# A hybrid attention and RWKV-7 layer on one core: the recurrence's chunk products on four quadrants of the array, and another road from the out projection into the FFN

## The chip, the cores and the metric

The kernel runs on one core of a Trainium2 chip. The metric is the device time of one execution in microseconds (us), lower is better; the time of a kernel is the median over its runs. Five engines work side by side and wait for one another through semaphores: TensorE (PE, with its weight loads listed apart as PEld), VectorE (DVE), ScalarE (ACT), GpSimd (POOL) and SyncE (SP), which issues most of the DMAs. Each engine goes through its own list of instructions in order, so an instruction that waits holds up everything behind it on that engine.

## The reference

One decoder layer over 1024 tokens of width 1024, all in float32. Half of the mixer's channels go through dilated attention (8 heads of 64), half through an RWKV-7 recurrence (8 heads of 64); both halves are joined, multiplied by an output matrix, normed and added to x; then comes an FFN from 1024 to 4096 and back.

```python
def step(state, inp):                       # RWKV-7, per head; state is 64 x 64
    r_t, w_t, k_t, v_t, kk_t, b_t = inp
    sa = einsum('bhij,bhj->bhi', state, kk_t)
    state = state * w_t[:, :, None, :] - sa[..., None] * b_t[:, :, None, :] + v_t[..., None] * k_t[:, :, None, :]
    return state, einsum('bhij,bhj->bhi', state, r_t)
...
mixed = concatenate([attn, rw], axis=-1) @ w_out
x = x + rms_norm(mixed, norm_mix_post)
h = rms_norm(x, norm_ffn_pre)
f = square(relu(h @ w_ffn_up)) @ w_ffn_down
x = x + rms_norm(f, norm_ffn_post)
```

where `rms_norm(x, g) = x / sqrt(mean(x*x) + 1e-6) * g`.

## The kernel before, in words

**Products.** A product of the projections is three matmuls (`mm3`: high times high, low times high, high times low), whose operands are split into a high and a low part; ACT writes the high part and DVE subtracts for the low one. `mm` records every matmul, so most matmuls of the program stand under one line (L47; L49 in the changed kernel). The small products of the recurrence are plain float32 matmuls, which the array runs as more than one instruction each.

**Projections and recurrence, 80 to 444 us of the span.** The sequence is cut into 16 chunks of 64 tokens, and the 8 RWKV heads are taken as 4 pairs; a pair's two heads lie in the two halves of the 128 partitions (`own[0]`, `own[1]`). Each pair goes through four jobs: `norms` (key norms, into the bank `pst`), `pre_pair` (decays, the chunk matrices N from the product `pN`, L436, and the spill of N), `subst` (solves small triangular blocks on DVE and writes them to `z_d`) and `merge` (L496): it loads Z from `z_d` (L502), transposes it to X (L503), multiplies N by X (`qu1`, L511) and the result W by Z (`qu2`, L519), merges again in 32x32 blocks (`qu3`, `qu4`), and stores to `zp_d` (L538), which `unit_e` needs later. `pN`, `qu1` and `qu2` are 32 products of 64x64 by 64x64 for each pair. In each, one head's operands and result lie in the upper half of the partitions, the other's in the lower: of the four 64x64 quadrants of the array the two on the diagonal take turns. After the pairs come eight units of 128 tokens: `unit_ab` and `unit_e` prepare the matrices, and `unit_c` (L624 on) walks the chunks one after the other, `O` from HV, then VU on ACT (L635), `O` from VU, then HV for the next chunk on DVE (L641, L642). That walk is serial.

**What sets the order there.** The six big projections (`z_k`, `z_r`, `z_v` for the recurrence, `z_aq`, `z_ak`, `z_av` for attention) are cut into 24 slabs of 48 matmuls. They are independent of the recurrence and are laid between its steps as filler. A planner, `drive` (L754), writes the order of PE and SP: it keeps a clock `now`, adds a cost for each step of a job (the first number of each `yield`) or 0.7 for three filler matmuls, and lets a job's next step in when its due time is past; due times come from the table `WAIT` or the default behind the `yield`. The last slabs (`aq3`, `ak3`, `av3`) may only start after the last chunk. DVE, ACT and POOL are ordered by the scheduler of the tile framework, by priority.

**Out projection and FFN, 618 us on.** The out projection goes by 8 token blocks of 128 (`half_mm`, 24 matmuls each half, into `pm`). `mix_x1` takes a block's norm, adds x, takes the next norm and scales (`yg`); `mix_h2` transposes yg on PE into `h2t` and writes high and low parts to `HB` and the sums `T1` to `T4`, four operands of a Strassen-like FFN: products of weight blocks with HB go to banks X and Y, later ones with T2, T1, T3 and T4 to X, Y and Z. Each weight block (`up_raw`, tile `wr`, 3 buffers) is loaded by SP and split by `split_w`; `up_rest` makes weight sums s21 and s34 on DVE. The last block of tokens (`pm7`, `y7`, `yg7`, `h2t7`) ends the out projection, and the third FFN product `X2` needs it. `rstd1` is the norm: a square root on ACT, then a reciprocal and one Newton step on DVE.

Of the kernel before, what the change touches and what calls it, by code (L numbers as in the profile page):

```python
# [1 line left out]

# [38 lines left out]
def hybrid_kernel(tc, x, par, cst, strip, win, wup_lora, gup, gnwb, grow, wout, wup, wdown, out, dbg=None):  # L41
# [22 lines left out]
    with (  # L64
# [29 lines left out]
        eps1 = cp.tile([P, 1], F32, name="eps1")  # L94
        A.activation(eps1, eps, AF.Sqrt)

        def rstd1(y, ssum, nm, more=eps, more_v=-0.5 * NORM_EPS):
# [6 lines left out]
            V.tensor_tensor(m, y, y, OP.mult)
            V.tensor_tensor(m, m, v_, OP.mult)
# [390 lines left out]
        def merge(p):  # L496
# [4 lines left out]
            for h in range(2):  # L501
                nc.sync.dma_start(Z[own[h]], d_full(zd, h))  # L502
# [1027 lines left out]
```

## Time and profile before

| | us |
|---|---|
| median of 3 runs (lowest, highest) | 1339.01 (1337.86, 1342.17) |
| the profiled execution's own time | 1342.16 |
| its span | 1338.3 |
| PE busy, share of the span | 1283.8 (96%) |
| DVE busy | 902.5 (67%) |
| ACT busy | 627.8 (47%) |
| POOL busy | 40.9 (3%) |
| granted TensorE clock, mean | 0.989 |

The span runs from the first to the last recorded event; the execution's time is 3.9 us longer. Stages in the span: x and first norm to about 47 us, small projections, then the pairs with projections as filler from 80 to 305 us, the units to 444, the last slabs to 473, attention to 618, out projection to about 710, FFN up to 1045, FFN down and the final norm to the end. PE is busy nearly all the time, so what it is given to do is read as closely as where it waits.

### The profile page before, as it was taken

How to read it: one execution, taken by the hardware profiler on the slowest of the kernel's cores; microseconds unless marked ns; L12 is line 12 of the kernel's file. 1: busy time of each engine (PE TensorE's matmuls, PEld its weight loads, DVE VectorE, ACT ScalarE, POOL GpSimd, SP SyncE). 2: the span in 40 equal slices, each digit the busy share in tenths (PEclk: the TensorE clock that was granted, in tenths of full speed). 3: DMA queues.
4: the chain of work that ended last, by engine and by line, in shares of the span. 5: the costliest groups of instructions: out<-in, count | busy, mean ns of one | idle time of the engine just before them, and what ended most of it. 6: DMA issues, size and time to landing. Idle time of an engine off the chain costs nothing.

```text
span 1338.3 us, 23569 instructions
## 1 busy us (share of the span) xinstructions
PE 1283.8 (96%) x9360; PEld 1060.0 (79%) x9360; DVE 902.5 (67%) x1648; ACT 627.8 (47%) x1029; POOL 40.9 (3%) x59
## 2 busy tenths in 40 slices
PE   6899999999989989999998999999999999999997
PEld 5677888878777878787886888888888888888876
DVE  7867657632677657655879977667766776445586
ACT  7653324233455267765656443434344344443443
POOL 0000000000000000000000000000000002000211
PEclk9999989999989989999999999999999999999999
DMA  7346746877585586502433544454457984346554
GB/s 259 116 173 171 193 119 186 245 209 228 177 250 168 188 270 183 149 25 96 152 106 136 177 164 147 140 168 151 148 189 238 348 326 161 104 133 200 189 197 180
DMA packets 163757, 239.48 MB, mean 179 GB/s; under 512 B 52192, under 2 KB 89312, under 8 KB 163648
## 3 DMA queue, kind: packets, MB, share of 16 engines
q1 hardware_dynamic: 154304, 212.81, 49.8%
q10 hardware_dynamic: 8064, 20.98, 4.7%
q0 software_dynamic: 1280, 4.20, 0.8%
q8 instruction: 73, 1.20, 0.4%
q14 instruction: 36, 0.29, 0.1%
HBM read 160.85 MB, written 77.09 MB: 178 GB/s over the span
## 4 chain that ended last, share of the span: by engine, by line
PE 74%; DVE 10%; DMA 9%; ACT 5%; issue 2%; SPq 1%; DVEq 0%; ACTq 0%
PE X L47 12%; PE dX L47 8%; PE Z L47 6%; PE pm L47 6%; PE dZ L47 5%; PE dY L47 3%; PE z_aq L47 3%; PE z_r L47 3%; PE Y L47 3%; PE z_v L47 3%; PE z_ak L47 2%; PE pT L909 2%; PE po L47 2%; PE pS L47 2%; PE z_av L47 2%
## 5 line engine op out<-in xcount | busy, mean ns | idle before, releaser
L47 PE MATMUL dX<-wow,wou 128*128 128x512 f32 x768 | 176.3, 390 | 2.4 <-DVE wow L1181 2.1
L47 PEld LDWEIGHTS dX<-wow,wou 128*128 128x128 f32 x768 | 143.8, 188 | 34.3 <-DVE wow L1181 3.8
L47 PE MATMUL dZ<-wow,wou 128*128 128x512 f32 x384 | 87.4, 389 | 0.0
L1180 ACT ACTIVATE wow<-wd 128x1024 fp32r<-128x1024 f32 x40 | 42.3, 1060 | 88.7 <-PE dZ L47 29.7
L47 PEld LDWEIGHTS dZ<-wow,wou 128*128 128x128 f32 x384 | 72.1, 188 | 15.0
L1181 DVE TENSOR_TENSOR wou<-ur,wou 128x1024 fp32r<-128x1024 f32 x56 | 71.8, 1283 | 7.2 <-ACT wou L1180 7.0
L1181 DVE TENSOR_TENSOR wow<-wd,wow 128x1024 fp32r<-128x1024 f32 x40 | 49.2, 1232 | 33.8 <-ACT wow L1180 33.4
L1180 ACT ACTIVATE wou<-ur 128x1024 fp32r<-128x1024 f32 x56 | 58.6, 1049 | 21.4 <-DMA ur<-u_d 14.1
L897 DVE CUSTOM_DVE_ANT_0 S<-pS,stripT 128x512 f32<-128x512 f32 (+3 forms) x64 | 37.7, 588 | 34.7 <-PE pS L47 33.1
L899 ACT ACTIVATE S<-S,mn 128x128 f32<-128x128 f32 (+7 forms) x64 | 49.4, 772 | 15.8 <-DVE mn L897 15.3
L1268 ACT ACTIVATE r<-u 128x512 f32<-128x512 f32 x48 | 30.1, 626 | 52.4 <-DVE u L1266 52.3
L909 PE MATMUL pT<-cst,S 128*128 128x128 f32 x288 | 44.8, 284 | 7.1 <-ACT PT L911 6.0
L47 PE MATMUL pm<-WO,mxr 128*128 128x512 f32 x192 | 49.2, 400 | 0.8 <-DVE mxr L977 0.8
L1181 DVE TENSOR_TENSOR wow<-TK,wow 128x1024 fp32r<-128x1024 f32 x16 | 20.8, 1301 | 38.9 <-ACT wow L1180 38.9
L47 PE MATMUL Z<-HB,wo 128*128 128x512 f32 x192 | 46.1, 389 | 0.0
L1452 POOL TENSOR_TENSOR E<-E,gpF 128x512 f32<-128x512 f32 x12 | 21.1, 1771 | 806.5 <-DMA xf<-x_d 639.7
L47 PE MATMUL pm<-WO,mxa 128*128 128x512 f32 x192 | 45.8, 394 | 0.0
L47 PE MATMUL z_aq<-hT,wh_aq 128*128 128x512 f32 x128 | 45.5, 407 | 0.0
L47 PE MATMUL X<-HB,wo 128*128 128x512 f32 x180 | 43.6, 390 | 1.6 <-ACT HB L1039 1.6
L47 PE MATMUL z_av<-hT,wh_av 128*128 128x512 f32 x128 | 45.1, 409 | 0.0
L909 PEld LDWEIGHTS pT<-cst,S 128*128 128x128 f32 x288 | 33.6, 144 | 14.5 <-ACT PT L911 10.5
L47 PE MATMUL z_r<-hT,wh_r 128*128 128x512 f32 x128 | 44.8, 408 | 0.0
(393 smaller groups left out, 3093.4 us busy)
## 6 DMA issues: line engine op xcount, KB each, us to landing
ur<-u_d SPq DMA_DIRECT2D x56, 512.0 KB, 4.3
wd<-in_wdown_dram SPq DMA_DIRECT2D x40, 512.0 KB, 4.3
u_d<-S SPq DMA_DIRECT2D x64, 256.0 KB, 2.1
u_d<-u SPq DMA_DIRECT2D x48, 256.0 KB, 2.2
wr_upa<-in_wup_dram SPq DMA_DIRECT2D x16, 512.0 KB, 3.6
wr_upb<-in_wup_dram SPq DMA_DIRECT2D x16, 512.0 KB, 4.0
TK<-in_wdown_dram SPq DMA_DIRECT2D x16, 512.0 KB, 7.6
x<-in_x_dram SPq DMA_DIRECT2D x8, 512.0 KB, 6.9
```

The costliest lines, as they stand in the source:

```text
L47: return PE.matmul(o, lhsT, rhs, start=start, stop=stop, skip_group_check=True)
L897: V.tensor_tensor_reduce(Sx[:, lo:hi], pS[:, :hi - lo], stripT[:, so:so + hi - lo], 1.0, 3e38 if k == 0 else mn[:, 0:1], OP.add, OP.min, a ...
L899: A.activation(Sx[:, :w], Sx[:, :w], AF.Exp, scale=-1.0, bias=mn[:, nbk - 1:nbk], accum_out=at[p, "den"][:, i, h:h + 1])
L909: PE.transpose(pt[:, j], Sx[:, (4 * k + j) * P:(4 * k + j + 1) * P], ident)
L1180: A.activation(w[:, 0, 0:n], raw, AF.Copy)
L1181: E.tensor_tensor(w[:, 1, 0:n], raw, w[:, 0, 0:n].bitcast(F32), OP.subtract)
L1268: A.activation(r, src, AF.Relu)
L1452: G.tensor_tensor(e, e, gn[n], OP.mult)
```

## The change

It has two halves. In the **recurrence**:

- A new helper `turned` issues the products of `pN`, `qu1` and `qu2` two chunks at a time. An even chunk's two heads use the diagonal quadrants as before; for an odd chunk, one of the operands or the result lies in the other half of the partitions, so the other two quadrants are used. The results go to two banks, one for even and one for odd chunks.
- So odd chunks of N and X lie in the other half. N is spilled by four DMAs of half the size instead of two (`d_half`). Z is loaded by four, and two more load a copy `Zo` of the odd chunks in their own half; the copy has the buffer tag `HX` that `subst` uses for its scratch tile. The mask of N is four DVE operations of half the size, and W is evacuated by ACT (even) and DVE (odd) instead of ACT alone.
- The sums for the key norms and the bonus (`pst`, `pb`) are issued through `mm_h`, which splits each product by output columns into two halves of 64.
- The planner has other costs for these steps and another `WAIT` table.

From the **out projection to the FFN**:

- `rstd1` needs three DVE operations instead of four.
- `mix_x1` multiplies by the gain ahead of the norm, works in halves of 512, and scales `yg` half on ACT, half on DVE. `mix_h2` saves copies (T3, T4) with two ACT instructions in its first half and needs fewer DVE operations in its second.
- The transposes of block ORD[6] are laid inside the last block's out projection, after 18 of its 24 matmuls.
- Several weight splits and sums are held by `issue_after` until named instructions of block 7's or block 6's norm have been issued: W1[1], W1[2], `up_rest(0)`, and the early parts of T.
- For the first FFN block the sums s34, the low parts w3 and w4, and the low part of T4 go to GpSimd.

```diff
-WAIT = {'mrg1.0': 26.0, ... 'ab1.0': 4}
+WAIT = {'mrg1.0': 26.0, ... 'H3': 1.0}
...
-    def rstd1(y, ssum, nm, more=eps, more_v=-0.5 * NORM_EPS):
+    V.tensor_scalar(eps4, eps, 0.25, None, op0=OP.mult)
+    def rstd1(y, ssum, nm, more=eps4, more_v=0.25 * NORM_EPS):
         n = ssum.shape[1]
         sq_, v_, m = (sm.tile([P, 2], F32, name=f"r1{c_}_{nm}", tag="r1" + c_, bufs=4)[:, :n] for c_ in "svm")
-        A.activation(sq_, ssum, AF.Sqrt, scale=1.0 / D, bias=more)
-        V.tensor_scalar(v_, ssum, -0.5 / D, more_v, op0=OP.mult, op1=OP.add)
-        V.reciprocal(y, sq_)
-        V.tensor_tensor(m, y, y, OP.mult)
-        V.tensor_tensor(m, m, v_, OP.mult)
-        V.scalar_tensor_tensor(y, m, 1.5, y, OP.add, OP.mult)
+        A.activation(sq_, ssum, AF.Sqrt, scale=0.25 / D, bias=more)
+        V.tensor_scalar(v_, ssum, 0.25 / D, more_v, op0=OP.mult, op1=OP.add)
+        V.reciprocal(m, sq_)
+        if n == 1:
+            V.scalar_tensor_tensor(m, m, v_, sq_, OP.mult, OP.add)
+        else:
+            V.tensor_tensor(m, m, v_, OP.mult)
+            V.tensor_tensor(m, m, sq_, OP.add)
+        V.reciprocal(y, m)
...
-                mm(pst[:, 8 * f + 2 * t:8 * f + 2 * t + 2], sq[:, t * P:(t + 1) * P], bone)
+                mm_h(pst[:, 8 * f + 2 * t:8 * f + 2 * t + 2], sq[:, t * P:(t + 1) * P], bone)
...
+    def turned(pq, f, lhsT, rhs, rows):
+        for cc in range(0, 8, 2):
+            for r in range(2):
+                for h in range(2):
+                    i = own[h ^ (r & rows)]
+                    mm(pq[r][own[h ^ (r & (1 - rows))], 4 * f + cc // 2], lhsT(cc, r)[i], rhs(cc, r)[i])
...
-            pN = bank(f"pN{p}_{f}", "w", bufs=2)
-            for cc in range(8):
-                for h in range(2):
-                    mm(pN[own[h], cc], bk[own[h], cc, 0, :], ar[own[h], cc, 0, :])
-            V.tensor_tensor(N[:, 8 * f:8 * f + 8], pN, maskn.unsqueeze(1).to_broadcast([P, 8, 64]), OP.mult)
-            yield 1.0, (3.0, 2.5)[f]
+            pN = [bank(f"pN{p}_{f}_{r}", "w", (P, 4, 64), 2) for r in range(2)]
+            turned(pN, 0, lambda cc, r: bk[:, cc + r, 0], lambda cc, r: ar[:, cc + r, 0], 0)
+            for r in range(2):
+                V.tensor_tensor(N[:, 8 * f + r:8 * f + 8:2], pN[r], maskn.unsqueeze(1).to_broadcast([P, 4, 64]), OP.mult)
+            yield 0.7, (3.2, 2.7)[f]
         for h in range(2):
-            nc.sync.dma_start(d_full(n_d[p % 2], h), N[own[h]])
+            for r in range(2):
+                nc.sync.dma_start(d_half(n_d[p % 2], h, r), N[own[h ^ r], r::2])
...
+        Zo = c8(t5(f"Zo{p}", "HX"))
         for h in range(2):
-            nc.sync.dma_start(Z[own[h]], d_full(zd, h))
+            for r in range(2):
+                nc.sync.dma_start(Z[own[h ^ r], r::2], d_half(zd, h, r))
+            nc.sync.dma_start(Zo[own[h]], d_half(zd, h, 1))
         V.transpose(fl(X), fl(Z))
         yield 0.0, 4.0
+        pq = [bank(f"qu1_{p}_{r}", "bc"[r]) for r in range(2)]
         for f in range(2):
-            fs = slice(8 * f, 8 * f + 8)
-            pu = bank(f"qu1_{p}_{f}", "bc"[f])
-            for cc in range(8):
-                for h in (0, 64):
-                    mm(pu[h:h + 64, cc], N[h:h + 64, 8 * f + cc], X[h:h + 64, 8 * f + cc])
-            A.activation(W[:, fs], pu, AF.Copy)
-        yield 2.4, 1.5
+            turned(pq, f, lambda cc, r: N[:, 8 * f + cc + r], lambda cc, r: X[:, 8 * f + cc + r], 1)
+        A.activation(W[:, 0::2], pq[0], AF.Copy)
+        V.tensor_copy(W[:, 1::2], pq[1])
+        yield 1.3, 1.9
+        pq = [bank(f"qu2_{p}_{r}", "bc"[r]) for r in range(2)]
         for f in range(2):
-            fs = slice(8 * f, 8 * f + 8)
-            pu = bank(f"qu2_{p}_{f}", "bc"[f])
-            for cc in range(8):
-                for h in (0, 64):
-                    mm(pu[h:h + 64, cc], W[h:h + 64, 8 * f + cc], Z[h:h + 64, 8 * f + cc])
-            V.copy_predicated(Z[:, fs], mk32.unsqueeze(1).to_broadcast([P, 8, 64]), pu)
+            turned(pq, f, lambda cc, r: W[:, 8 * f + cc + r], lambda cc, r: Zo[:, 4 * f + cc // 2] if r else Z[:, 8 * f + cc], 0)
+        for r in range(2):
+            V.copy_predicated(Z[:, r::2], mk32.unsqueeze(1).to_broadcast([P, 8, 64]), pq[r])
         V.transpose(fl(X), fl(Z))
-        yield 2.4, 4.0
+        yield 1.3, 4.4
...
+                if between and (n, k) == (1, BK):
+                    between()
...
+        hs = [slice(n * 512, n * 512 + 512) for n in range(2)]
+        for n in range(2):
+            V.tensor_tensor(y[:, hs[n]], src[n], gpM[:, hs[n]], OP.mult)
         V.tensor_tensor(st[:, 2:3], st[:, 2:3], st[:, 3:4], OP.add)
         rstd1(st[:, 4:5], st[:, 2:3], f"m{t}")
+        jh = mp.tile([P, D], BF, name=f"jh{t}", tag="jh", bufs=1)
+        yg = mp.tile([P, D], F32, name=f"yg{t}", tag="yg")
         for n in range(2):
-            ns = slice(n * 512, n * 512 + 512)
-            V.scalar_tensor_tensor(y[:, ns], src[n], st[:, 4:5], gpM[:, ns], OP.mult, OP.mult)
-        V.tensor_tensor(y, y, xt, OP.add)
+            ld = V.scalar_tensor_tensor(y[:, hs[n]], y[:, hs[n]], st[:, 4:5], xt[:, hs[n]], OP.mult, OP.add)
+            la = A.activation(jh[:, hs[n]], y[:, hs[n]], AF.Square, accum_out=st[:, (5, 7)[n]:(6, 8)[n]])
+        MX[t] = la, ld
         nc.sync.dma_start(x_d[tt, :], y)
-        jh = mp.tile([P, D], BF, name=f"jh{t}", tag="jh", bufs=1)
-        A.activation(jh, y, AF.Square, accum_out=st[:, 5:6])
+        V.tensor_tensor(yg, y, gF, OP.mult)
+        V.tensor_tensor(st[:, 5:6], st[:, 5:6], st[:, 7:8], OP.add)
         rstd1(st[:, 6:7], st[:, 5:6], f"h{t}")
-        yg = mp.tile([P, D], F32, name=f"yg{t}", tag="yg")
-        V.tensor_tensor(yg, y, gF, OP.mult)
-        A.activation(yg, yg, AF.Copy, scale=st[:, 6:7])
+        A.activation(yg[:, hs[0]], yg[:, hs[0]], AF.Copy, scale=st[:, 6:7])
+        V.tensor_scalar(yg[:, hs[1]], yg[:, hs[1]], st[:, 6:7], None, op0=OP.mult)
...
-            return last
-        B11, B21 = HB[0, 0].bitcast(F32), HB[1, 0].bitcast(F32)
-        V.tensor_tensor(f(T1), pt[0], B11[:, 0, :, qs], OP.subtract)
-        V.tensor_tensor(f(T1), f(T1), B11[:, 1, :, qs], OP.subtract)
+            with tc.issue_after(la.ins):
+                for q in range(2):
+                    A.activation(f((T3, T4)[q]), pt[q], AF.Copy)
+            return la, last
+        V.tensor_tensor(f(T1), pt[0], f(T3), OP.subtract)
         V.tensor_tensor(f(T2), pt[1], f(T1), OP.subtract)
         if between:
             between()
-        V.tensor_tensor(HB[1, 1][:, 1, :, qs], pt[1], HB[1, 1].bitcast(F32)[:, 0, :, qs], OP.subtract)
-        V.tensor_tensor(f(T3), f(T2), B11[:, 0, :, qs], OP.subtract)
-        V.tensor_tensor(f(T3), f(T3), B11[:, 1, :, qs], OP.subtract)
-        V.tensor_tensor(f(T4), B21[:, 0, :, qs], f(T2), OP.subtract)
-        V.tensor_tensor(f(T4), B21[:, 1, :, qs], f(T4), OP.add)
+        with (tc.issue_after(W2I[0].ins) if between else contextlib.nullcontext()):
+            V.tensor_tensor(HB[1, 1][:, 1, :, qs], pt[1], HB[1, 1].bitcast(F32)[:, 0, :, qs], OP.subtract)
+            V.tensor_tensor(f(T3), f(T2), f(T3), OP.subtract)
+            V.tensor_tensor(f(T4), f(T4), f(T2), OP.subtract)
...
+    last_h0 = lambda: h6s.append(mix_h2(ORD[6], ygs.pop(6)))
...
-        half_mm(ORD[i], pms[i], ax.pop(i), 0, i < 2, True)
+        half_mm(ORD[i], pms[i], ax.pop(i), 0, i < 2, True, last_h0 if i == 7 else None)
...
+        E = G if j == 0 else V
+        E.tensor_tensor(s34[:, h[0]], r1[:, h[0]], r2[:, h[0]], OP.subtract)
+        E.tensor_tensor(s34[:, h[1]], r1[:, h[1]], s21[:, h[0]], OP.subtract)
+        w3_ = split_w(s34, f"3_{j}", E)
+        w4_ = split_w(r2[:, h[1]], f"4_{j}", E)
...
-    for j in range(2):
-        W1[j] = split_w(up_raw(2 * j, f"e{j}"), f"1_{j}")
-    h6 = mix_h2(ORD[6], ygs.pop(6))
+    W1[0] = split_w(up_raw(0, "e0"), "1_0")
+    with tc.issue_after(h6s[0][0].ins), tc.issue_after(h6s[0][1].ins):
+        W1[1] = split_w(up_raw(2, "e1"), "1_1")
...
+    ea, ed = MX[ORD[7]]
+    raw = up_raw(4, "e2")
+    with tc.issue_after(ea.ins), tc.issue_after(ed.ins):
+        W1[2] = [stg.tile([P, D], F32R, name=f"w12{q}", tag=("wh", "wl")[q]) for q in range(2)]
+        A.activation(W1[2][0], raw, AF.Copy)
+        V.tensor_tensor(W1[2][1], raw, W1[2][0].bitcast(F32), OP.subtract)
+        ws0 = up_rest(0, up_raw(0, "a0"), up_raw(1, "b0"))
+        for k, v in TS.items():
+            A.activation(v[1][:, :, early_], v[0][:, :, early_], AF.Copy)
         t_low(2, early_, V)
...
+            t_low(k, slice(0, 512), V if k == 3 else G)
...
```

Three places in the order of instructions. The first is the PE list at `qu1` of pair 0; `qu1_0_0` is the bank of the first half of the chunks before, and of the even chunks in the changed kernel. Before:

```order
L47 MATMUL z_k3_0_1572<-hT_106,wl_k3_1434 128x512
L47 MATMUL z_k3_0_1572<-hT_106,wh_k3_1433 128x512
L47 MATMUL qu1_0_0_1591<-X0_1268,N0_981 64x64 x16
L47 MATMUL qu1_0_1_1609<-X0_1268,N0_981 64x64 x16
L47 MATMUL z_k3_0_1572<-hT_106,wh_k3_1433 128x512
```

In the changed kernel; the last two rows are the first of sixteen that alternate:

```order
L49 MATMUL z_k3_0_1593<-hT_108,wh_k3_1476 128x512
L49 MATMUL pst2_1607<-cst_75,sq2_0_1608 64x2 x8
L49 MATMUL pst2_1607<-cst_75,sq2_1_1618 64x2 x8
L49 MATMUL qu1_0_0_1644<-X0_1267,N0_966 64x64 x2
L49 MATMUL qu1_0_1_1645<-X0_1267,N0_966 64x64 x2
```

The count of products is the same, 32; they change banks after every two, and the norm sums of pair 2 are 16 products of 64 columns instead of 8 of 128.

The second is the PE list at the end of the units, around the first product of unit 7 (E7 is `unit_e`, O7 the chunk walk, z_av2 filler, z_aq3 the first slab that has to wait for the last chunk). Before, the start of the last unit:

```order
L47 MATMUL O6_1_4758<-VU6_4496,TR0_1025 64x64 x16
L47 MATMUL E7_1_4839<-TR1_1026,Zp7_4499 64x128 x8
L47 MATMUL z_av2_0_4689<-hT_106,wh_av2_4082 128x512
L47 MATMUL z_av2_0_4689<-hT_106,wl_av2_4083 128x512
L47 MATMUL z_av2_0_4689<-hT_106,wh_av2_4082 128x512 x2
L47 MATMUL z_av2_0_4689<-hT_106,wl_av2_4083 128x512
L47 MATMUL z_av2_0_4689<-hT_106,wh_av2_4082 128x512
L47 MATMUL O7_0_4860<-HV7_4683,T1_7_4649 64x64 x16
```

In the changed kernel the whole of the last unit:

```order
L49 MATMUL O6_1_4894<-VU6_4652,TR0_1039 64x64 x16
L49 MATMUL E7_0_4975<-TR1_1040,Zp7_4655 64x128 x8
L49 MATMUL O7_0_4987<-HV7_4831,T1_7_4797 64x64 x16
L49 MATMUL E7_1_5004<-TR1_1040,Zp7_4655 64x128 x8
L49 MATMUL O7_0_4987<-VU7_4834,TR1_1040 64x64 x16
L49 MATMUL O7_1_5040<-HV7_4831,T1_7_4797 64x64 x16
L49 MATMUL O7_1_5040<-VU7_4834,TR1_1040 64x64 x16
L49 MATMUL z_aq3_0_5114<-hT_108,wh_aq3_5102 128x512
```

Before, filler stands between all steps of the last unit; in the changed kernel there is none. Over all units, between the first O group and the last, PE's list holds 231 filler matmuls before and 189 in the changed kernel.

The third is ACT's list around the second norm of the last token block (`r1s_h7` is its square root, `w120` the split of the third FFN weight block, which waits for the load of `wr_upe2`). Before:

```order
L1180 ACTIVATE wo2_0_8249<-s21_0_8245 128x1024
L1021 ACTIVATE jh7_8141,st7_8122<-y7_8124 128x1024
L1180 ACTIVATE wo3_0_8254<-s34_0_8246 128x1024
L101 ACTIVATE r1s_h7_8143<-st7_8122,eps_74 128x1
L1180 ACTIVATE wo4_0_8257<-wr_upb0_8243 128x512
L1242 ACTIVATE w120_8262<-wr_upe2_8260 128x1024
L1025 ACTIVATE yg7_8152<-yg7_8152,st7_8122 128x1024
L1039 ACTIVATE HB11_7305<-h2t7_1_8271 128x4x128
```

In the changed kernel:

```order
L1035 ACTIVATE jm7_8260,st7_8259<-pm7_1_8176 128x512
L106 ACTIVATE r1s_m7_8267<-st7_8259,eps4_79 128x1
L1045 ACTIVATE jh7_8275,st7_8259<-y7_8261 128x512 x2
L1274 ACTIVATE w120_8363<-wr_upe2_8361 128x1024
L106 ACTIVATE r1s_h7_8284<-st7_8259,eps4_79 128x1
L1278 ACTIVATE T2h_8356<-T2_7416 128x4x384
L1278 ACTIVATE T1h_8357<-T1_7417 128x4x384
L1051 ACTIVATE yg7_8276<-yg7_8276,st7_8259 128x512
```

The copies T1h to T4h and the splits of w2, w3 and w4 have left the place ahead of this norm; the split of w12 now stands ahead of the square root, and ahead of it only the two squares of y7.

More of the change, by code (lines that the diff above doesn't have):

```diff
@@ L1 @@
+import contextlib
 import math
+import contextlib
 import numpy as np
@@ L360, in d_full, with d_half @@
             return bass.AP(tensor=v.tensor, offset=v.offset, ap=[[64, 64], [4160, 16], [1, 64]])
+        def d_half(d, h, r):
+            v = d[h * 16 + r:h * 16 + 16]
+            return bass.AP(tensor=v.tensor, offset=v.offset, ap=[[64, 64], [8320, 8], [1, 64]])
         def d_blk(d):
@@ L537, in merge @@
                 for c_ in range(2):
-                    nc.sync.dma_start(zp_d[:, :, c_, p, h, :].rearrange("n r m -> r n m"), X[own[h], c_::2])
+                    nc.sync.dma_start(zp_d[:, :, c_, p, h, :].rearrange("n r m -> r n m"), X[own[h ^ c_], c_::2])
             yield 0.0, 0.0
@@ L989, in half_a, with half_mm @@
             return half_t(t, m, "a", tag)
-        def half_mm(t, pm, mx, k0, first, last):
+        BK = 2
+        MX = {}
+        def half_mm(t, pm, mx, k0, first, last, between=None):
             for n in range(2):
@@ L1038, in mix_h2 @@
             for q in range(h, 2):
-                A.activation(HB[q, h][:, 0, :, qs], pt[q], AF.Copy)
+                la = A.activation(HB[q, h][:, 0, :, qs], pt[q], AF.Copy)
             if h == 0:
@@ L1153, in hybrid_kernel @@
         pms[1] = pm_new(ORD[1], "bc")
+        h6s = []
+        last_h0 = lambda: h6s.append(mix_h2(ORD[6], ygs.pop(6)))
         for i in range(8):
@@ L1175, in bank @@
             return ps.tile([P, 512], F32, name=nm, tag=tag, bufs=2 if tag in "zw" else 1)
+        W2I = []
         def split_w(raw, nm, E=V, pool=None):
@@ L1180, in split_w @@
             A.activation(w[:, 0, 0:n], raw, AF.Copy)
-            E.tensor_tensor(w[:, 1, 0:n], raw, w[:, 0, 0:n].bitcast(F32), OP.subtract)
+            low = E.tensor_tensor(w[:, 1, 0:n], raw, w[:, 0, 0:n].bitcast(F32), OP.subtract)
+            if nm == "2_0":
+                W2I.append(low)
             return w
@@ L1226, in hybrid_kernel @@
         early_, late = slice(0, 384), slice(384, 512)
-        for k, v in TS.items():
-            v.append(tp.tile([P, 4, 512], F32R, name=f"T{k}h", tag="woA", bufs=4))
-            A.activation(v[1][:, :, early_], v[0][:, :, early_], AF.Copy)
         def t_low(k, qs, E):
@@ L1235, in hybrid_kernel @@
         new_low = lambda k: TS[k].append(h2p.tile([P, 4, 512], F32R, name=f"T{k}l", tag="T", bufs=5))
+        for k, v in TS.items():
+            v.append(tp.tile([P, 4, 512], F32R, name=f"T{k}h", tag="woA", bufs=4))
         new_low(2)
-        with tc.issue_after(h6.ins):
-            t_low(2, early_, V)
-        ws0 = up_rest(0, up_raw(0, "a0"), up_raw(1, "b0"))
-        raw = up_raw(4, "e2")
-        W1[2] = [stg.tile([P, D], F32R, name=f"w12{q}", tag=("wh", "wl")[q]) for q in range(2)]
-        A.activation(W1[2][0], raw, AF.Copy)
-        V.tensor_tensor(W1[2][1], raw, W1[2][0].bitcast(F32), OP.subtract)
+        ea, ed = MX[ORD[7]]
[5 more added lines that the diff above has]
+            ws0 = up_rest(0, up_raw(0, "a0"), up_raw(1, "b0"))
+            for k, v in TS.items():
+                A.activation(v[1][:, :, early_], v[0][:, :, early_], AF.Copy)
+            t_low(2, early_, V)
         def t2_late():
@@ L1247, in t2_late @@
             t_low(2, late, V)
-        mix_h2(ORD[7], ygs.pop(7), t2_late)
+        with tc.high_priority(offset=PRI[0]):
+            mix_h2(ORD[7], ygs.pop(7), t2_late)
         up_first(2, W1[2])
@@ L1253, in hybrid_kernel @@
             new_low(k)
-            t_low(k, slice(0, 512), V)
+            if k == 1:
+                with tc.high_priority(offset=PRI[1]):
+                    t_low(k, slice(0, 512), V)
+            else:
+                t_low(k, slice(0, 512), V if k == 3 else G)
         HT = {k: v[1:] for k, v in TS.items()}
@@ L1280, in first_out @@
             def first_out(j):
-                s1 = keep(f"s1_{j}", XB[j])
+                with (tc.high_priority(offset=PRI[1]) if j == 0 else contextlib.nullcontext()):
+                    s1 = keep(f"s1_{j}", XB[j])
                 return evac(f"11_{j}", s1s[j], s1)
@@ L1405, in final @@
                 else:
-                    rstd1(st[:, t, 3:4], st[:, t, 0:1], f"f{t}", st[:, t, 4:5], st[:, t, 5:6])
+                    rstd1(st[:, t, 3:4], st[:, t, 0:1], f"f{t}", st[:, t, 4:5], st[:, t, 4:5])
                 for n in range(2):
```

12 lines of the change are left out of this document (4 added, 8 removed).

## The prediction

> **What bounds the kernel now.** I read the page's totals first, then the chain of waits by engine.
>
> ```profile
> span 1338.3 us, 23569 instructions
> PE 1283.8 (96%) x9360; PEld 1060.0 (79%) x9360; DVE 902.5 (67%) x1648; ACT 627.8 (47%) x1029; POOL 40.9 (3%) x59
> PE 74%; DVE 10%; DMA 9%; ACT 5%; issue 2%; SPq 1%; DVEq 0%; ACTq 0%
> ```
>
> PE is busy 96% of the span and carries 74% of the chain that ended last. So two things can move the end: less time for what PE is given, or fewer and shorter idle stretches of PE. Next I read busy time by stretch: the pairs, the units, the out projection up to the third FFN product, and two short stretches inside the units.
>
> ```profile
> core 0: us, PE busy (x) PEld busy (x) DVE busy (x) ACT busy (x) POOL busy (x), PEclk, DMA share, GB/s
> 80.00:304.98 224.98, 222.17 (x2241) 184.44 (x2239) 144.73 (x319) 80.81 (x136) 7.55 (x21) 0.98 0.65 183
> 304.98:444.12 139.14, 130.78 (x1801) 105.35 (x1800) 88.14 (x203) 63.72 (x109) 3.46 (x7) 0.98 0.66 199
> 618.00:725.55 107.55, 100.08 (x496) 82.68 (x494) 84.96 (x195) 62.85 (x116) 0.00 (x0) 1.00 0.38 130
> 392.00:396.00 4.00, 1.82 (x34) 1.64 (x32) 3.93 (x9) 0.59 (x1) 0.54 (x1) 0.81 0.68 217
> 396.00:400.00 4.00, 4.00 (x31) 2.91 (x31) 1.39 (x3) 2.30 (x4) 0.00 (x0) 0.50 0.60 212
> ```
>
> In the pairs PE idles 2.81 us of 224.98: there a shorter PE instruction shortens the kernel nearly one for one, because filler follows at once. In the units it idles 8.4 us, up to the third FFN product 7.5 us. The last two rows show a second cost of idling: after a stretch in which PE worked 1.82 of 4 us, the granted clock is 0.50 for the next four.
>
> **The quadrants.** The timeline of PE gives the price of the batches. The second number is the duration with the pipeline's tail, so I take the distance to the start of the next row.
>
> ```profile
> 155.45 2.08 PE L47 MATMUL qu<-X,N 64*64 64x64 f32 x64
> 157.46 0.50 PE L47 MATMUL z_k<-hT,wh_k 128*128 128x512 f32 x1
> ...
> 166.05 1.20 PE L47 MATMUL qu<-X,N 32*32 32x32 f32 x64
> 167.18 0.50 PE L47 MATMUL z_k<-hT,wh_k 128*128 128x512 f32 x1
> ...
> 90.33 1.84 PE L47 MATMUL pst<-cst,sq 128*128 128x2 f32 x16
> 92.03 0.96 PE L47 MATMUL g<-ghl,sgs 128*128 128x512 f32 x3
> ...
> 389.83 1.15 PE L47 MATMUL O<-VU,TR 128*64 128x64 f32 x32
> 390.91 0.83 PE L47 MATMUL p<-AR,K 64*128 64x128 f32 x10
> ```
>
> A batch `qu` of 64 instructions, 64x64 on two quadrants, takes 157.46 - 155.45 = 2.01 us, 31 ns each. With twice as many quadrants at work it could take half, 1.0 us. What I do not know is whether the array takes instructions that fast. The nearest row is the 32x32 batch: also 64 instructions, 167.18 - 166.05 = 1.13 us. I take 1.13. Four pairs with pN, qu1 and qu2 make 12 batches: 12 x (2.01 - 1.13) = **-10.6 us**. Bounds: 0, if the added quadrants wait for one another, and 12 x 1.0 = -12.
>
> A batch's two heads already write one bank from different halves of the rows at 31 ns each; the O batch, which uses all rows and two halves of the columns, takes (390.91 - 389.83) / 32 = 34 ns. So sharing a bank shows no price here. The Trainium skill, "TensorEngine Tiling (Array Packing)", section "Restrictions and Gotchas", says that different row tiles cannot access the same PSUM bank at once, and after the change both banks still take results from both row halves. By that rule the batches would gain nothing; the 31 ns speak against it, and I keep it as a rival.
>
> **Norm sums.** `pst` is 16 instructions of 128 columns and 2 moving ones, 92.03 - 90.33 = 1.70 us. Split by columns it is 32 instructions in two column halves, for which O's 1.08 us is the nearest row; 0.1 more for one more change of tile shape. Eight batches (pst and pb, four pairs): 8 x (1.70 - 1.18) = **-4.2 us**. Bounds: 0 and 8 x 1.1 = -9.
>
> **Z's chain on SP.** What becomes later is Z: N goes out in two more DMAs, and the transpose now waits for the fifth of six loads instead of the second of two. The view of tile Z and the timeline around pair 3's loads:
>
> ```profile
> L502 SPq DMA_DIRECT2D Z<-z_d x8: 592/664/1857, 127.9 to 273.8; - x8
> ...
> 272.73 2.88 SPq L502 DMA_DIRECT2D Z<-z_d  x2
> 279.60 1.25 DVE L503 STREAM_TRANSPOSE X<-Z 128x1024 f32<-128x1024 f32 x1 [1.42 <-DMA Z<-z_d]
> ...
> 237.53 1.15 PE L47 MATMUL pN<-ar,bk 64*64 64x64 f32 x32
> 283.14 2.08 PE L47 MATMUL qu<-X,N 64*64 64x64 f32 x64
> ```
>
> At 0.664 us for issuing a piece, five more are 3.3 us. Pair 3 is the tightest: the chain from pN's end (238.61 at most) to the transpose's end (280.85) is 42.2 us, now 45.5. In the changed order I count 43.7 us of PE work between that pN and qu1, at the trace's 0.227 us for a 128x512 matmul and the batches above. That leaves a stall of some **+2 us**. Bounds: 0, if half-size pieces land sooner, and +8, if each piece costs what the slow ones do (1.44 us, half of 2.88) and pair 2 stalls as well. The masks and W's evacuation, which DVE shares now, lie under filler; so does the wait of the next `subst` for the buffer HX. Without that cover each would cost a 64x512 operation, 0.67 us.
>
> **The units.** Moving filler is free by itself: 231 - 189 = 42 matmuls, 42 x 0.227 = 9.5 us, go ahead of the units. What it uncovers is the serial walk. Which waits ended there, and how one looks:
>
> ```profile
> PE O L47 <- DVE HV L642: 3.4, 3, 2.2
> PE O L47 <- DMA T<-ar_d: 2.4, 3, 1.2
> PE ptk L580 <- ACT TR L599: 2.1, 4, 0.5
> PE O L47 <- ACT VU L635: 0.3, 1, 0.3
> ...
> 394.26 1.83 PE L47 MATMUL O<-HV,T 128*64 128x64 f32 x32 [2.18 <-DVE HV L642]
> ```
>
> A step from O to the next O through HV costs 2.18 us of idle PE with nothing between. In the changed order three halves of the walk have the VU product right behind the HV product (about 0.9 us each, the 0.59 us of ACT's copy and the semaphores on both sides), and the last unit has no filler at all: one HV step of 2.18 and two VU steps less the 1.0 us of E7_1 in one of them. That is 3 x 0.9 + 3.3 = 6.0 more; due times that the table moved later may save a third of it, so +4. The last unit then is a stretch like 392 to 396, followed by the half clock: about 4 us at 0.50, +2. Together **+6 us**. Bounds: 0, if the new due times pay for all, and 15 HV steps x 2.18 = 33 less the 3.4 already there, +29. The Trainium skill, "TensorE: Matmul & The Clock Gate", section "What's actually happening", gives an idle window of about 3.4 us for the gate to close; here 2.18 us inside a thin stretch did it, so I go by the row; by the page's window no single gap of the last unit would be long enough, and the term would be +4.
>
> **Out projection to FFN.** PE's two waits there, the loads and the operations behind them:
>
> ```profile
> 710.09 3.29 PE L47 MATMUL X<-HB,wo 128*128 128x512 f32 x12 [1.60 <-ACT HB L1039]
> 724.70 1.18 PE L1037 MATMUL h2t<-cst,yg 128*128 128x128 f32 x8 [3.16 <-ACT yg L1025]
> ...
> 717.97 0.42 SPq L1186 DMA_DIRECT2D wr_upe<-in_wup_dram  x1
> 722.55 1.06 ACT L1242 ACTIVATE w<-wr_upe 128x1024 fp32r<-128x1024 f32 x1 [2.08 <-DMA wr_upe<-in_wup_dram]
> 723.51 1.13 ACT L1025 ACTIVATE yg<-yg,st 128x1024 f32<-128x1024 f32 x1
> ...
> 711.42 1.75 DVE L1233 TENSOR_TENSOR T2l<-T,T2h 128x1536 fp32r<-128x1536 f32 x1
> ...
> 716.36 1.21 DVE L1018 TENSOR_TENSOR y<-y,xr 128x1024 f32<-128x1024 f32 x1
> ...
> 739.36 2.28 DVE L1233 TENSOR_TENSOR T4l<-T,T4h 128x2048 fp32r<-128x2048 f32 x1
> 744.00 0.62 PE L47 MATMUL X<-T4h,wo 128*128 128x512 f32 x2
> ```
>
> At most 1.60 + 3.16 = 4.8 us can go. y7 was done at 716.36 + 1.21 = 717.57 and comes some 3.8 us sooner: the T2l of 1.75 us that stood inside its norm and three weight sums on DVE, 0.68 us each, are held back. But the next norm does not follow. In ACT's list its square root stands behind the split of w12, which waits for `wr_upe2`; that load has the buffer of y7's residual, so it starts when y7 is done and takes 722.55 - 717.97 = 4.58 us. From y7 at about 713.8: load to 718.4, split to 719.5; DVE, in order, makes the low part (1.2), then the norm (0.5), then T2l (1.75), then its half of yg (0.7): about 723.7 for the transposes against 724.70. I take **-1 us**; bounds -4.8 and, with the next paragraph, +6.
>
> On POOL, T4l is new. How a POOL operation and DVE get on shows the final stage:
>
> ```profile
> 1287.02 0.14 DVE L104 TENSOR_TENSOR r1m_f<-stF 128x1 f32<-128x1 f32 x1
> 1287.27 3.53 POOL L1452 TENSOR_TENSOR E<-E,gpF 128x512 f32<-128x512 f32 x2 [1.51 <-ACT jf L1393]
> 1289.58 1.25 DVE L105 TENSOR_TENSOR r1m_f<-r1m_f,r1v_f 128x1 f32<-128x1 f32 x1
> ```
>
> A DVE operation on 128x1, 0.14 us alone, took 1.25 behind a 128x512 pair on POOL: a two-input operation waits for the other engine's. T4l is four times 128x512, 3.53 / 2 x 4 = 7.1 us, and T3l and other low parts on DVE could stand behind it while PE needs T3 some 5.5 us ahead of T4. At full price T3l comes 7.1 us later, less 1 us that it had in hand, +6; but PE reads T4 only at 744.00, 19 us after h2t7, and the 2.28 us that T4l took on DVE leave DVE's list, so I take 0. The shorter norm saves one 0.14 us operation in the last block's tail: **-0.2 us** with its semaphore.
>
> **The sum.** -10.6 - 4.2 + 2 + 6 - 1 - 0.2 = -8.0. From the profiled execution, 1342.16 us (span 1338.3 and 3.9 around), that gives 1334.2. That execution is the highest of the three shown and 3.15 above their median of 1339.01, so I forecast **1331.0 us**.
>
> **Rivals.**
>
> - Bank sharing or issue keeps the new quadrants apart: the term of -10.6 is zero, -8.0 + 10.6 = +2.6, about 1341.6. For it: the trace has no four-quadrant batch of 64x64. Against: 31 ns in one bank, and 17.7 ns for an instruction of the 32x32 batch. Chance 0.06.
> - Slower: the walk through the units lies bare. Filler has gone from between its steps, and the planner's costs are lower, so it believes that steps end sooner; at 2.18 for all 15 HV steps the units cost +29 instead of +6, some 1354. It decides from the point at which the units lose 17 us or more, 1.2 us for each HV step, where the whole comes out over 0.3% slower. For it: in the pairs filler covers little, since PE idles 2.81 us there, and what is spent there is missing in the units. Against: 189 filler matmuls are still 43 us for 31 gaps. Chance 0.10.
> - POOL's operation holds DVE at full price: +6 and no gain at the transition, +7 on the forecast, 1338. For it: the 1.25 us row; against: the slack ahead of T4. Chance 0.10.
> - The waits vanish: units 0 instead of +6, Z's chain 0 instead of +2, the transition -4.8 instead of -1: -19.8, 1319.2. For it: due times can move what stalls; against: the order of ACT around w12. Chance 0.14.
>
> The forecast has 0.60, its own range 1325 to 1337. A measurement here can tell about 0.3%, 4.0 us, from no change: 1335.0 to 1343.0. Faster: 0.53 of the forecast's 0.60, 0.14 and 0.03 of POOL's: 0.70. Slower: 0.10 of the units' and 0.01 of the first. Same: 0.19. The range 1320 to 1342 leaves out most of the slower case and the far end of the faster one.
>
> **What would show it.** The batches pN, qu1 and qu2 at about 1.1 us per 64 instructions, pst at 1.2. Idle PE before qu1 of pairs 2 and 3, ended by the transpose. Idle PE between 305 and 444 us near 12 instead of 8.4, and a half clock at the first aq3 slab. ACT waiting for `wr_upe2` with the square root behind it, h2t7 only about 1 us sooner. If the batches keep 2.01 us or the units idle over 25 us, the forecast falls; if h2t7 follows its predecessors without a wait, my reading of the queue on ACT was wrong.

## The result and the profile after

The changed kernel took 1345.81 us (median of 10 runs, 1342.73 to 1351.39), the kernel before 1338.05 beside it (1333.02 to 1343.37): a ratio of 1.0052, 95% interval 1.0034 to 1.007. It is slower by half a per cent, where I forecast faster by 0.6%. The profiled execution took 1343.36 us.

The page of the changed kernel: totals, the chain of waits by engine, and the groups of FFN down.

```profile
span 1341.2 us, 23913 instructions
PE 1277.3 (95%) x9488; PEld 1038.9 (77%) x9488; DVE 906.9 (68%) x1640; ACT 626.6 (47%) x1049; POOL 53.4 (4%) x64
PE 55%; DVE 11%; DMA 9%; ACT 4%; issue 3%; SPq 1%; DVEq 0%; ACTq 0%
L49 PE MATMUL dX<-wow,wou 128*128 128x512 f32 x768 | 180.7, 395 | 1.1 <-DVE wow L1212 1.0
L49 PE MATMUL dZ<-wow,wou 128*128 128x512 f32 x384 | 89.9, 395 | 0.0
```

The same two groups in the kernel before:

```profile
L47 PE MATMUL dX<-wow,wou 128*128 128x512 f32 x768 | 176.3, 390 | 2.4 <-DVE wow L1181 2.1
L47 PE MATMUL dZ<-wow,wou 128*128 128x512 f32 x384 | 87.4, 389 | 0.0
```

PE's busy time fell by 6.5 us, although the quadrants and norm sums alone should take more than twice that away. The two groups show where much of it went: the matmuls of FFN down, which the diff does not touch, are 5 to 6 ns longer each, together 6.9 us of busy time, and they wait no longer than before. In a stretch of 100 us in the middle of FFN down (columns: busy time and number of instructions for PE, PEld, DVE, ACT, POOL, then the granted clock, the DMA share and GB/s) the kernel before issued

```profile
1160.00:1260.00 100.00, 100.00 (x443) 82.81 (x442) 55.29 (x56) 42.47 (x50) 7.65 (x4) 1.00 0.51 166
```

and the changed kernel

```profile
1160.00:1260.00 100.00, 100.00 (x430) 80.33 (x429) 53.30 (x50) 40.89 (x48) 7.50 (x4) 1.00 0.49 160
```

13 matmuls fewer, at the same clock of 1.00 and with no idle time. From the start of one matmul to the start of the next, a `dZ` there took 226.7 ns before and takes 233.3 ns now.

Read by landmarks, the profiled execution of the changed kernel was ahead all the way to the FFN and lost it there. Times in the span, from the PE timeline:

| | before | changed | lead |
|---|---|---|---|
| end of the last projection slab | 487.2 | 478.8 | 8.4 |
| end of attention | 616.6 | 609.9 | 6.7 |
| end of the out projection | 707.6 | 702.3 | 5.3 |
| first FFN product | 710.1 | 702.1 | 8.0 |
| end of the last transposes h2t | 725.9 | 715.0 | 10.9 |
| end of FFN up | 1022.5 | 1019.1 | 3.4 |
| end of FFN down | 1331.1 | 1334.6 | -3.5 |

(The list of stages ahead of the prediction lets the last slabs end at 473 and FFN up at 1045; the trace says 487.2 and 1022.5.) Each column is one execution, and executions differ early on: in the traces of e2, e3, e4, e9 and e11 below, which keep the recurrence of before, the last slab ends between 478.0 and 487.0, and in e8's, which has the new one, at 485.0. The upper rows can't tell what the recurrence brought; the runs below do.

Its gain is made in batches like these two, of norm sums and of `qu1` on four quadrants, on the changed kernel's PE timeline:

```profile
147.44 1.10 PE L49 MATMUL pst<-cst,sq 128*64 128x2 f32 x32
148.47 1.16 PE L49 MATMUL qu<-X,N 64*64 64x64 f32 x64
149.56 0.50 PE L49 MATMUL z_k<-hT,wh_k 128*128 128x512 f32 x1
```

1.03 us and 1.09 us, against 1.70 and 2.01 before. What it cost stands in the waits, of the pairs first, then of the units:

```profile
PE qu L49 <- DVE X L526: 2.4, 1, 2.4
...
PE O L49 <- DVE HV L661: 4.4, 6, 1.5
PE O L49 <- ACT VU L654: 2.9, 4, 0.8
PE ptk L599 <- ACT TR L618: 2.1, 4, 0.5
PE O L49 <- issue: 2.1, 1, 2.1
PE E L49 <- DMA Zp<-zp_d: 1.5, 1, 1.5
PE E L49 <- ACT TR L592: 1.1, 1, 1.1
```

The units' waits sum to 14.1 us against 8.2. The stall before `qu` is in pair 3, at 273.07 us. The end of the last unit, which has no filler now:

```profile
428.24 1.15 PE L49 MATMUL O<-HV,T 128*64 128x64 f32 x32 [2.06 <-issue]
430.08 1.98 PE L49 MATMUL O<-VU,TR 128*64 128x64 f32 x32 [0.68 <-ACT VU L654]
431.98 0.80 PE L49 MATMUL z_aq<-hT,wh_aq 128*128 128x512 f32 x1
```

The last O batch takes 1.98 us instead of 1.15 and the first slab matmul 0.80 instead of 0.39 to 0.50: the granted clock is 0.50 there, until 436.3 us. This trace is a mild case: over 300 to 490 us the mean granted clock is 0.96 in it and 0.93 to 0.96 in the traces of e1, e5, e6, e7, e8 and e12, which have its order table, against 0.96 to 0.99 in the kernel before, e2, e3, e4, e9 and e11. What that costs in time, no run tells apart.

Between out projection and FFN, the two waits of before (1.6 us for HB, 3.2 us for yg) are gone but for 0.7 us, and others have come. Waits, then what VectorE and GpSimd did there, then SP's loads:

```profile
PE X L49 <- DVE u L1307: 2.1, 1, 2.1
PE Z L49 <- DVE T1l L1264: 2.1, 1, 2.1
PE h2t L1064 <- DVE yg L1052: 0.7, 1, 0.7
PE X L49 <- DVE T2l L1264: 0.7, 1, 0.7
...
718.71 0.68 DVE L1079 TENSOR_TENSOR HB<-h2t,HB 128x512 fp32r<-128x512 f32 x1
719.31 2.31 DVE L1264 TENSOR_TENSOR T2l<-T,T2h 128x512 fp32r<-128x512 f32 x1
721.55 1.79 DVE L1080 TENSOR_TENSOR T<-T,T 128x512 f32<-128x512 f32 x1
...
718.56 2.50 POOL L1212 TENSOR_TENSOR wo<-s,wo 128x1024 fp32r<-128x1024 f32 x1 [1.67 <-ACT wo L1211]
721.03 1.77 POOL L1212 TENSOR_TENSOR wo<-wr_upb,wo 128x512 fp32r<-128x512 f32 x1
...
693.90 2.31 SPq L1219 DMA_DIRECT2D wr_upe<-in_wup_dram  x2
707.35 0.33 SPq L1047 DMA_DIRECT2D x_d<-y  x1
```

T2l on VectorE, 0.68 us by its form, lasts 2.31: until 721.6, just behind the end of GpSimd's low part of w3 at 721.06. The next operation, 1.79 us long, ends behind GpSimd's low part of w4, and T1l comes after both. T4l does the same to the first weight sum of the next FFN block:

```profile
729.68 4.94 POOL L1264 TENSOR_TENSOR T4l<-T,T4h 128x2048 fp32r<-128x2048 f32 x1 [6.89 <-issue]
730.08 5.09 DVE L1227 TENSOR_TENSOR s<-wr_upb 128x512 f32<-128x512 f32 x1
737.03 0.72 PE L49 MATMUL X<-T4h,wo 128*128 128x512 f32 x2 [2.10 <-DVE u L1307]
```

That sum, again 0.68 us by its form, takes 5.09 us, until just behind T4l's end, and the `u` for which PE waits 2.1 us stands behind it in VectorE's list.

The load of `wr_upe2` went out with that of `wr_upe1` at 693.9, 13 us ahead of the store of y7.

### The profile page after: what moved, and what is told of

The parts are those of the page before. It is cut to its first block, busy times and chain, and to the rows that moved or that the text cites. A ratio compares the mean times of both kernels' runs of the same rounds, so it can differ in the third digit from the quotient of the medians.

```text
span 1341.2 us, 23913 instructions
## 1 busy us (share of the span) xinstructions
PE 1277.3 (95%) x9488; PEld 1038.9 (77%) x9488; DVE 906.9 (68%) x1640; ACT 626.6 (47%) x1049; POOL 53.4 (4%) x64
## 4 chain that ended last, share of the span: by engine, by line
PE 55%; DVE 11%; DMA 9%; ACT 4%; issue 3%; SPq 1%; DVEq 0%; ACTq 0%
PE X L49 10%; PE dX L49 8%; PE pm L49 6%; PE dZ L49 5%; PE Z L49 5%; PE dY L49 3%; PE Y L49 2%; PE pT L928 2%; PE pS L49 2%; PE po L49 2%; PE z_ak L49 2%; PE z_aq L49 2%; DMA bv<-v_d 2%; PE O L49 2%; DMA wd<-in_wdown_dram 2%
## 5 line engine op out<-in xcount | busy, mean ns | idle before, releaser
L49 PE MATMUL dX<-wow,wou 128*128 128x512 f32 x768 | 180.7, 395 | 1.1 <-DVE wow L1212 1.0
L49 PE MATMUL dY<-wow,wou 128*128 128x512 f32 x192 | 45.0, 395 | 0.0
L49 PE MATMUL z_k<-hT,wh_k 128*128 128x512 f32 x128 | 43.5, 397 | 1.4 <-DVE z L242 1.4
L49 PE MATMUL z_ak<-hT,wh_ak 128*128 128x512 f32 x128 | 43.7, 405 | 0.0
```

The source lines that it names most:

```text
L49: return PE.matmul(o, lhsT, rhs, start=start, stop=stop, skip_group_check=True)
```

## The experiments

**First question: why is untouched work slower?** The diff puts one new tile into the constants, `eps4`, 4 bytes in each partition. In the built program it takes 32 bytes and moves every tile behind it on that side of the memory by 32; the tiles of the pools on the right side stay. In FFN down the moving operand (`wow`) lies on the left and the stationary one (`wou`) on the right, so their distance changes; in the projections both lie left, in the products of HB with the weights both lie right. The pace had changed in the groups whose distance had: FFN down, the products with T1h to T4h (left) and the half of the out projection with `mxr`; the products Y with HB kept 226.7 ns. Four runs tested that.

```diff
 # e1: the changed kernel; every tile where it was
-eps = cp.tile([P, 32], F32, name="eps")[:, 0:1]
+eps_ = cp.tile([P, 32], F32, name="eps")
+eps = eps_[:, 0:1]
-eps4 = cp.tile([P, 1], F32, name="eps4")
+eps4 = eps_[:, 8:9]
 # e2 (w = 8) and e3 (w = 16): the kernel before
+pad = cp.tile([P, w], F32, name="pad")
+V.memset(pad, 0.0)
 # e4: e2, and on the other side
+pad2 = tp.tile([P, 8], F32, name="pad2")
+nc.gpsimd.memset(pad2[0:1, 0:1], 0.0)
```

> The changed kernel with eps4 kept in a spare column of the tile eps instead of a tile of its own, so that every tile of the program stands at the address it had before the change. Theory (addresses): the new tile of 4 bytes takes 32 bytes and moves all tiles on its side of the memory by 32; where the moving and the stationary operand of a 128x512 matmul then differ by 32 modulo 64 bytes, one takes 233 ns instead of 227. That is 1296 matmuls of FFN down x 6.6 ns = 8.6, some 700 of FFN up x 4.5 = 3.2, and 192 of the out projection x 5 = 1.0: 12.8 us. Expected about 1333, FFN down at 227 ns a matmul. Rival (the chip's own drift, and the GpSimd sums): the slower pace has nothing to do with addresses, 1346 stays.

> The kernel before with an unused tile of 32 bytes added behind eps1, nothing else. Theory (addresses): +12.8 us, about 1351, FFN down at 233 ns a matmul where operands differ by 32 modulo 64. Rival (drift, GpSimd): 1338, no change.

> The kernel before with an unused tile of 64 bytes in the same place. Theory (addresses modulo 64): 1338, no change, 227 ns. Rival (any shift of tiles, or a tile more, costs): about 1351.

> The kernel before with an unused tile of 32 bytes on both sides of the memory, so that moving and stationary operands of nearly all big matmuls are both at 32 modulo 64. Theory (the difference between the two operands counts): 1338, 227 ns. Rival (an operand at 32 modulo 64 costs by itself): FFN down at 233 ns or more, the projections too, 1351 or more.

Measured: e1 1333.35 us, ratio to the kernel before 0.9948 (0.9923 to 0.9972); e2 1349.33, 1.0063 (1.0035 to 1.0091); e3 1343.02, 1.004 (1.0014 to 1.0067); e4 1353.73, 1.0106 (1.0068 to 1.0144). The stretch of FFN down in e1, then in e2, e3 and e4:

```profile
1160.00:1260.00 100.00, 100.00 (x442) 82.79 (x442) 55.44 (x52) 41.49 (x49) 7.65 (x4) 1.00 0.51 169
```

```profile
1160.00:1260.00 100.00, 100.00 (x431) 80.30 (x430) 53.65 (x54) 41.48 (x49) 7.51 (x4) 1.00 0.47 154
```

```profile
1160.00:1260.00 100.00, 100.00 (x439) 82.05 (x438) 55.27 (x56) 41.50 (x49) 7.62 (x4) 1.00 0.49 158
```

```profile
1160.00:1260.00 100.00, 100.00 (x439) 82.05 (x438) 54.15 (x55) 42.39 (x51) 7.61 (x4) 1.00 0.47 154
```

e1 and e2 settle the cause: with the tile's place alone undone the changed kernel is faster than the kernel before, and an unused tile of 32 bytes brings that kernel to the pace of the changed one. (Its loss of 0.0063, 8.4 us, with an interval from 4.7 to 12.2, is less than the 12.8 I expected; the cause is better known than its size.) But the theory was wrong in its number. 64 bytes are not free, and e3 and e4 have the same pace in every group, though all addresses differ: e3's left tiles stand 64 further, e4's left ones 32 further and its right ones 32 the other way. What they share is the distance, 64. So it is the distance of the two operands that counts, and its free multiples are larger than 64. In the kernel before every such distance is a multiple of 256 bytes. Two more runs, the changed kernel with `eps4` as a tile of 256 bytes, and the kernel before with 128 more:

```diff
 # e7: the changed kernel
-eps4 = cp.tile([P, 1], F32, name="eps4")
+eps4 = cp.tile([P, 64], F32, name="eps4")[:, 0:1]
 # e11: the kernel before
+pad = cp.tile([P, 32], F32, name="pad")
```

> The changed kernel as it is, but with eps4 in a tile of 256 bytes instead of 4. In the trials with 32 and 64 bytes the pace of a matmul followed the distance of its two operands; distances of 0 and 256 modulo 512 took 227 ns. Theory (a distance that is a multiple of 256 is free): 227 ns in FFN down and up, about 1333. Rival (the free distances are those of the kernel before alone): 228 to 236 ns, 1340 or more.

> The kernel before with an unused tile of 128 bytes, so that the operands' distance in FFN down and in the products with T is 128 modulo 256. Theory A (multiples of 256 alone are free): a pace of 229 ns or more. Theory B (multiples of 128 are free as well): 227 ns and no change of the time.

e7: 1333.78 us, 0.995 (0.9926 to 0.9973). e11: 1346.03 us, 1.0059 (1.0042 to 1.0076). The stretch in e7, then in e11:

```profile
1160.00:1260.00 100.00, 100.00 (x443) 82.81 (x442) 54.15 (x51) 42.71 (x50) 7.66 (x4) 1.00 0.53 173
```

```profile
1160.00:1260.00 100.00, 100.00 (x430) 80.44 (x429) 52.85 (x55) 41.03 (x48) 7.49 (x4) 1.00 0.50 163
```

So a multiple of 256 is free, 128 is not, and any of the tried distances between them costs. From start to start of consecutive matmuls in the traces, with the shift of the left tiles against the right ones:

| shift, bytes | kernels | FFN down, ns | X with T-high, ns | pm with mxr, ns | Y with HB (both right), ns |
|---|---|---|---|---|---|
| 0 | before, e1 | 226.7 | 227 | 228 | 226.7 |
| 32 | changed, e2 | 233.3 | 232 | 233 | 226.7 |
| 64 | e3, e4 | 228.9 | 236 | 233 | 226.8 |
| 128 | e11 | 233.4 | 229 | 232 | 226.7 |

The slow pace also reaches neighbours. In the changed kernel the T-low products, whose operands both lie right, take 230 to 232 ns between the T-high ones, and of the twelve products X or Z with HB behind a group of T products the first four take 228 to 236 and the rest 226 or 227. So it is the pace of a run of matmuls that changes, and not only that of the one whose operands stand apart. That the same shift costs FFN down and T differently, 228.9 and 236 ns at 64, these runs don't explain, and the mechanism behind it all is open. e4 is 10 us slower than e3 at the same pace of its matmuls; where those went is open too (their two traces are 4.6 us apart, of which 4.2 stand at the first FFN product already).

**Second question: what is the recurrence worth?** e8 is the kernel before with the recurrence's part of the diff alone. e5 is e1 with the odd chunks in their own half again, so that only the number of quadrants differs; e12 takes back `mm_h` for the norm sums, on the base of e6 (below).

```diff
 # e5, on e1
-    i = own[h ^ (r & rows)]
-    mm(pq[r][own[h ^ (r & (1 - rows))], ...)
+    i = own[h]
+    mm(pq[r][own[h], ...)
 # and N[own[h], r::2], Z[own[h], r::2], X[own[h], c_::2] in the DMAs
 # e12, on e6
-mm_h(pst[...], ...)      mm_h(pb[...], ...)
+mm(pst[...], ...)        mm(pb[...], ...)
```

> The kernel before with the change of the recurrence alone (four quadrants, norm sums by column halves, the new costs and WAIT table), so without a new tile in the constants. Theory: it brings nearly all of the gain that the change has at the old addresses, 6.6 us at the end of the projections, about 1333. Rival (the gain is made at the out projection and the FFN): 1337 or more.

> The changed kernel at the old addresses (eps4 in a spare column), with the odd chunks put back into their own half: the same banks, order, number of DMAs and WAIT table, only the products use the two diagonal quadrants again. Theory (four quadrants run side by side): pN, qu1 and qu2 take 2.0 us for 64 instructions instead of 1.09, 12 x 0.9 = 11 us more, about 1344 against 1333. Rival (the time is filled elsewhere, the chains' latency sets the pairs): less than half of it, under 1339.

> The changed kernel at the old addresses with the sums on VectorE, with pst and pb as eight products of 128 columns again. Theory (column halves run side by side): 8 x (1.70 - 1.03) = 5.4 us more than 1330.6, about 1336. Rival (hidden in the pairs' chains): 1332 or less.

e8: 1333.4 us, 0.9948 (0.9924 to 0.9972), all of the gain that e1 has. e5: 1342.15 us, 1.0001 (0.9978 to 1.0024); against e7, which was measured beside it and differs from e1 only in where the tile lies, 8.4 us slower, with intervals that do not overlap. Its batch of 64:

```profile
150.48 2.08 PE L49 MATMUL qu<-X,N 64*64 64x64 f32 x64
152.49 0.50 PE L49 MATMUL z_k<-hT,wh_k 128*128 128x512 f32 x1
```

2.01 us, as before the change, with the banks and the alternation of the changed kernel: the quadrants run side by side, and that is the gain. The 12 batches save PE 11 us; some 2 of them seem to be given back, and PE's idle time between 80 us and the first O product is 4.3 us in e7's trace and 1.8 in e5's. e12: 1333.8 us, 0.9963 (0.994 to 0.9985), against e6's 0.9925, so 0.0038 x 1339 = 5.1 us. The intervals of the two overlap, so the size is uncertain; it agrees with 8 x 0.67 = 5.4.

**Third: GpSimd's sums.** e6 is e1 with the sums and low parts of the first FFN block and T4l on VectorE; e9 is the kernel before with the second half of the change alone, GpSimd's sums included.

```diff
 # e6, on e1
-E = G if j == 0 else V
+E = V
-t_low(k, slice(0, 512), V if k == 3 else G)
+t_low(k, slice(0, 512), V)
```

> The changed kernel at the old addresses, with the sums s34, the low parts w3, w4 and T4l of the first FFN block back on VectorE. Theory (a GpSimd operation and a VectorE operation with two inputs exclude each other): the waits of PE for T2l, T1l and u (1.6 + 2.1 + 0.6 us) shrink below 2 us, about 1331, and no VectorE operation there is longer than its usual 0.68 us for 128x512. Rival (VectorE is the bottleneck and GpSimd relieves it): the waits grow, 1336 or more.

> The kernel before with the second half of the change alone (shorter norm, held splits and sums, sums on GpSimd), eps4 in the spare column, so that addresses stay. Theory: what it takes away (1.6 + 3.2 us of waits for the last block's transposes) comes back as waits for T2l, T1l and u behind GpSimd's operations: within 3 us of the kernel before. Rival (it brings its waits as a whole): 4.8 us faster or more.

e6: 1330.63 us, 0.9925 (0.99 to 0.9949), the fastest kernel of this study and faster than both. PE's waits at that place in e1, and then in e6 with VectorE's T2l:

```profile
PE Z L49 <- DVE T1l L1265: 2.1, 1, 2.1
PE X L49 <- DVE T2l L1265: 1.6, 1, 1.6
PE X L49 <- DVE u L1308: 0.6, 1, 0.6
```

```profile
PE Z L49 <- DVE T1l L1265: 1.5, 1, 1.5
PE X L49 <- DVE wo L1213: 0.8, 1, 0.8
...
720.42 0.68 DVE L1265 TENSOR_TENSOR T2l<-T,T2h 128x512 fp32r<-128x512 f32 x1
```

4.3 us of waits became 2.3, a little above the 2 that I expected, and T2l takes 0.68 us again. FFN up from its first to its last product takes 309.4 us instead of e1's 312.4. Against e7, beside it, e6 is 3.2 us faster, but their intervals overlap, so the size rests on the traces. e9: 1335.89 us, 0.9979 (0.9958 to 0.9999), 2.5 us below the kernel before, at the edge of what can be told from none: what the second half takes away, 4.8 us of waits, comes back as 5.3 us of waits in its trace (for u, T1l, T2l and yg).

**Fourth: the order table.** e10 is e6 with the `WAIT` table of the kernel before.

> The changed kernel at the old addresses with the sums on VectorE, with the WAIT table of the kernel before (the new step costs stay); 231 filler matmuls between the first and the last O group, as before the change, rather than 189, is what one would hope for. Theory (the filler taken from the units costs some 5 us of idle there, and the new table does not pay it back): the units' idle falls, about 1327. Rival (the table fits the new steps, the old one lets steps in at the wrong times): 1332 or more.

e10: 1356.39 us, 1.013 (1.0093 to 1.0166), 26 us slower than e6. Its waits between 80 and 320 us:

```profile
PE qu L49 <- DVE X L527: 5.9, 2, 5.4
PE pv L700 <- DVE vc L707: 3.8, 1, 3.8
PE g L49 <- DVE N L457: 3.5, 1, 3.5
PE pN L49 <- DVE bk L453: 1.7, 1, 1.7
```

My theory fell. In the order it has 219 filler matmuls in the units, where the changed kernel has 189 (the kernel before, counted in the same way, 228, three fewer than the part on the change says). But the table is made of due times on a clock that adds up the step costs, and with the new costs the old due times seem to let steps in before their inputs are there: 5.4 us before one `qu`, and from 80 to 300 us PE is busy for 202.4 us where it is for 214.6 in e6. At the end of attention it is 28 us behind e6, 639.9 against 611.8.

## Why the prediction was wrong, point by point

- **Shorter norm, -0.2 us.** This is the term that failed. I costed the new `rstd1` by its instructions and took its constant `eps4` for nothing. The tile cost 12.5 us by the medians (1345.81 against e1's 1333.35), 0.0104 x 1339 = 13.9 by the ratios; their intervals together leave about 10 to 18. In the trace FFN down went from 308.3 to 315.3 us (e1 against changed), FFN up from 312.4 to 316.6, of which some is waits. The sum held a hidden assumption: that work which the diff does not touch keeps its duration. With the tile out of the way, e1 is 2.4 us from the forecast of 1331.0, though not every term below came out for its reason.
- **The quadrants, -10.6 us.** Right: 1.09 us for a batch where I took 1.13. The first rival fell: both banks take results from both row halves, and the batch takes little more than half of its former time.
- **Norm sums, -4.2 us.** Right and a little small: 1.03 us instead of 1.18 makes -5.4; e12 fits, within its interval.
- **Z's chain, +2 us.** Right: one stall of 2.4 us before `qu` of pair 3, ended by the transpose (X, L526).
- **The units, +6 us.** Right in kind, too small: the waits, 14.1 instead of 8.2 us, are +5.9 where I took +4, and the half clock at the first aq3 slab, 6.8 us long in this trace where I took 4, adds another 2 to 3; it came although no gap there was longer than 2.06 us. (The working's own terms for the last unit add up to 3.0, not 3.3.) The slower rival, the walk laid bare, did not come; e10 shows that the risk was in the table, and in the pairs rather than in the units.
- **Out projection to FFN, -1 us.** The number is near e9's -2.5, the reasoning was wrong twice, in opposite directions. The square root did not stand behind a load: I carried the place of `wr_upe2` over from the trace of before, behind the store of y7, although in the changed list of SP it had moved ahead of it. So h2t ended 10.9 us sooner, of which 5.3 stood at the end of the out projection already: 5.6 by this stage, and not 1. And GpSimd's price, which I set to 0, was paid three times: at w3 and w4, on T2l and the operation behind it, and at T4l, which held not T3l but the next block's sum for 5.09 us; some 3 us by e6. That was the third rival's mechanism, mostly at other places. That the two errors nearly cancelled was luck.
- **The sum.** Recurrence and transition together came out near the forecast, -8.0 predicted, about -6 to -7 measured by e1, in part because the errors of single terms, a larger gain on the norm sums and larger losses in the units, stand against each other. The result lies outside the range through the one term that was not in it, and none of the rivals held it.
